# Down projection of eight hidden tiles as seven block products, with their rows kept whole, and a changed last stage

## The chip, the cores and the metric

The kernel runs on one core of one Trainium2 chip. The metric is the device time of one execution in microseconds (us). A core has five engines, each with its own queue that runs in order: TensorE (PE, matmuls into PSUM; PEld is its loading of weights), VectorE (DVE), ScalarE (ACT), GpSimd (POOL) and SyncE (SP, which issues most of the transfers from HBM). They wait for each other through semaphores. TensorE and its accumulators work on tiles of 128 partitions; an accumulator bank of PSUM holds 128x512 numbers of four bytes.

## What is computed

A two-layer trunk over 512 tokens with a model width of 1024. Each layer is a mixer and a gated feed-forward part, each behind an RMS norm and added to the residual. The change touches the feed-forward part of the second layer (layer 1) and the final norm behind it. The feed-forward part has a hidden width of 2816, which is 22 tiles of 128:

```python
def gated_conv_ffn(x, w_gate, w_up, conv_w, conv_b, w_down):
    g = jnp.einsum('bsd,df->bsf', x, w_gate)
    g = causal_dwconv3(g, conv_w) + conv_b
    up = jnp.einsum('bsd,df->bsf', x, w_up)
    return jnp.einsum('bsf,fd->bsd', jax.nn.silu(g) * up, w_down)
...
    h = h + gated_conv_ffn(hn, w_ffn_gate[layer], w_ffn_up[layer], ...)
return rms_norm(h, final_norm)
```

## The kernel before

*Precision.* Every matrix is held as two parts, a rounded high part and the low part that is left (`hi`, `lo`), and every product is three matmuls: high by high, high by low, low by high (`mm3`, L152, recorded at L153, L154 and L155). So each operand must be split. `parts` (L145) does it with a copy on ScalarE (L148) and a subtraction on VectorE (L149); `summed` (L135) does it without VectorE: ScalarE writes the negative of the rounded part (L139), a transfer issued by GpSimd adds the operand onto it in memory (L140), and ScalarE copies the high part (L142). `split` (L257) does the same for rows of activations (L260 on ScalarE, L262 on VectorE), `halves` (L677, recorded at L678 and L679) for sums.

*Rings.* A tile with a tag is one of a fixed number of buffers that are used in turn. Raw weights: four (`raw`, 128x1024, 512 KB each, fetched by SP at L129). Split weights: six (`whi`, `wlo`). Sums: three (`sum`). Activation parts: four (`ahi`, `alo`). Silu rows: three for odd tiles (`s`), two for even ones (`sq`). Whoever takes the next buffer waits until its last reader is done.

*Up projections.* Hidden tiles are taken in pairs f, f + 1; "pair f" below. The gate and up products of a pair are each computed by Strassen's scheme in Winograd's form on two by two blocks: 7 products for the gate and 7 for the up part (`products`, L721), 12 matmuls of 128x256 each (`multiply`, L531, recorded at L542). `prepare` (L681) fetches four raw tiles and makes the weights of all products: a11 is split directly, and s12 and s34 (for g and for u) are sums and differences of blocks which VectorE forms (L698 to L711) and `halves` splits; the fourth block goes through `summed`. The products' order is g1, u1, g5, g6, u5, u6, g2, g7, u2, u7, g4, g3, u4, u3: g1 and u1 need a11, g5 and g6 need s12g, u5 and u6 need s12u, and so on. Results leave PSUM by copies on ScalarE (L736) and adds on VectorE (L741, L746) into padded rows and a tile `kept`; then VectorE multiplies with the norm's factor (L756), convolves (L576), and multiplies silu's result with the up part (L760, L761, L766).

*Down projection.* The rows of four tiles, once split, are multiplied with their 512 columns of the down weights into four banks, one for each 128 tokens, 48 matmuls of 128x512 (`half_down`, L1107), and VectorE adds each bank onto y with the norm's factor (`add`, L1104). A list of steps says which half follows which pair:

```python
    STEPS = [(0, None, True), (2, (0, 2, 0), True), (4, (0, 2, 1), True)]
    for f in range(6, NF, 4):
        STEPS += [(f, (f - 4, f, 0), False), (f + 2, (f - 4, f, 1), f + 4 < NF)]
```
So in layer 1 TensorE runs pair 2, half of tiles 0 and 1, pair 4, their other half, pair 6, half of tiles 2 to 5, pair 8, their other half, pair 10, half of tiles 6 to 9, and so on to pair 20 and the other half of tiles 14 to 17.

*Last four tiles.* Tiles 18 to 21 use the seven-product scheme for the down part too: token halves by tile pairs on one side, tile pairs by column halves on the other. Weights: differences t1, t2 and two more in place (`less`), all seven split by `summed` (`put`). Rows: sums s1, s2 and two in place, each of the seven blocks split into the high and low tiles of the layer's input norm (`hg`), which are free by then. Each product is 12 matmuls of 128x512 for two groups of 128 tokens, recorded at L1204; products 1, 6, 7 and 4 share a bank `a` for each of the two groups, 5 and 3 a bank `e`, 2 has `b`. So the add onto y that reads a bank has to be done before the next product onto that bank begins.

*Order.* A scheduler moves instructions between program order and queue order by due times; `inorder` keeps some in program order, `behind` puts one behind another on its engine. After the last four tiles, the final norm is written out in order by hand: `taken` (a product and its add), `squared` (ScalarE, sum of squares), `halved`, `rooted`, `inverted` (the norm's factor of 128 tokens, on one column), `times` (rows by the norm's gain) and `scaled` (by the factor, and the transfer out).

## Time and profile before

| what | value |
| --- | --- |
| median of three runs | 988.8 us (988.59 to 989.36) |
| the profiled execution | 988.85 us |
| its span in the profile | 987.1 us |
| mean granted TensorE clock | 0.998 of full speed |
| layer 1's pairs 2 to 20 with their down halves | 658.3 to 958.3 us |
| the last four tiles' products, to the last matmul | 958.3 to 977.8 us |
| from there to the end of the span | 9.3 us |
| read from HBM, written | 98.42 MB, 2.10 MB |

The page has, among other parts, the busy time of every engine, the chain of waits that ended last, and groups of instructions by line. A line of a timeline gives an instruction's start in us from the span's start, its duration, engine, line in the kernel, operation, the tiles written and read, and in brackets how long its engine sat idle before it and what ended that. A line of busy time by stretch gives the stretch, its length, then busy time and number of instructions of each engine, the clock, the transfer engines' share and GB/s.

### The profile page before, as it was taken

To read this page: it belongs to the slowest core of one execution; us is meant where nothing else is said; L and a number is where in the kernel's file an instruction comes from. 1 tells how busy PE (TensorE), PEld (TensorE's weight loads), DVE (VectorE), ACT (ScalarE), POOL (GpSimd) and SP (SyncE) were. 2 spreads that over 40 slices of the span, in tenths; PEclk is the share of its full clock that TensorE was granted. 3 is DMA by queue.
4 is the path that set the end of the run, shared out by engine and by line. 5 is a ranking of instruction groups with operands and counts; after the bars stand their busy time and mean duration, and the time that the engine had idled before them with its cause. 6 is when DMAs were issued, how large, how long until landed. Compare 5 with 4: busy or idle time off the path is not lost.

```text
span 987.1 us, 15485 instructions
## 1 busy us (share of the span) xinstructions
PE 975.2 (99%) x6099; PEld 879.9 (89%) x6099; DVE 775.9 (79%) x1181; ACT 562.0 (57%) x843; POOL 112.0 (11%) x129
## 2 busy tenths in 40 slices
PE   9999999999999999999999999999999999999996
PEld 6788888999999999999889988889999999999985
DVE  5797458998788887886887765589987779777787
ACT  5623347755465654655488734576655456554675
POOL 2142022000000000000210001210000000000022
PEclk9999999999999999999999999999999999999999
DMA  7442225555465454653324623264565465445573
GB/s 248 131 150 85 86 86 128 135 137 157 129 150 133 132 142 129 150 130 108 126 64 120 198 69 106 55 140 128 150 166 133 130 149 147 119 135 135 161 151 116
DMA packets 87942, 129.32 MB, mean 131 GB/s; under 512 B 4309, under 2 KB 57789, under 8 KB 87869
## 3 DMA queue, kind: packets, MB, share of 16 engines
q1 hardware_dynamic: 78172, 98.69, 32.2%
q0 software_dynamic: 8208, 27.79, 15.5%
q10 hardware_dynamic: 1488, 1.84, 0.6%
q8 instruction: 48, 0.79, 0.3%
q14 instruction: 26, 0.20, 0.1%
HBM read 98.42 MB, written 2.10 MB: 102 GB/s over the span
## 4 chain that ended last, share of the span: by engine, by line
PE 85%; DVE 8%; ACT 2%; issue 1%; DMA 0%; POOL 0%; ACTq 0%; DVEq 0%
PE dn L153 3%; PE dn L154 3%; PE dn L155 3%; PE d L153 3%; PE d L154 3%; PE d L155 3%; PE oo L155 1%; PE oo L153 1%; PE oo L154 1%; PE oe L154 1%; PE oe L153 1%; PE oe L155 1%; PE u_20a L542 1%; PE u_18a L542 1%; PE u_16a L542 1%
## 5 line engine op out<-in xcount | busy, mean ns | idle before, releaser
L576 DVE SCALAR_TENSOR_TENSOR c<-rows,prm,c 128x512 f32<-128x512 f32 x88 | 64.1, 747 | 1.5 <-ACT c L574 1.4
L140 POOL DMA_DIRECT2D wlo_g<-raw_g x20 | 17.2, 859 | 387.4 <-ACT wlo_g L139 350.4
L153 PE MATMUL d<-a_hi,whi_d 128*128 128x512 f32 x144 | 56.1, 390 | 0.0
L153 PE MATMUL dn<-whi_dn,a_hi 128*128 128x512 f32 x144 | 56.1, 390 | 0.0
L154 PE MATMUL dn<-wlo_dn,a_hi 128*128 128x512 f32 x144 | 56.1, 390 | 0.0
L154 PE MATMUL d<-a_lo,whi_d 128*128 128x512 f32 x144 | 56.1, 390 | 0.0
L155 PE MATMUL d<-a_hi,wlo_d 128*128 128x512 f32 x144 | 56.0, 389 | 0.0
L155 PE MATMUL dn<-whi_dn,a_lo 128*128 128x512 f32 x144 | 56.0, 389 | 0.0
L679 DVE TENSOR_TENSOR wlo_s34u<-s34u,whi_s34u 128x1024 fp32r<-128x1024 f32 x20 | 24.5, 1224 | 25.5 <-ACT whi_s34u L678 25.5
L149 DVE TENSOR_TENSOR wlo_dn<-raw_dn,whi_dn 128x1024 fp32r<-128x1024 f32 x18 | 22.0, 1225 | 23.6 <-ACT whi_dn L148 23.4
L142 ACT ACTIVATE whi_u<-raw_u 128x1024 fp32r<-128x1024 f32 x21 | 22.2, 1055 | 31.6 <-PE d L154 17.5
L149 DVE TENSOR_TENSOR wlo_d<-raw_d,whi_d 128x1024 fp32r<-128x1024 f32 x18 | 22.0, 1224 | 19.5 <-ACT whi_d L148 19.5
L198 ACT ACTIVATE hgh<-h,prm 128x512 fp32r<-128x512 f32 x24 | 17.3, 722 | 35.1 <-DVE h L309 35.0
L140 POOL DMA_DIRECT2D wlo_u<-raw_u x21 | 18.1, 860 | 162.0 <-ACT wlo_u L139 83.7
L584 ACT ACTIVATE s<-c,prm 128x512 f32<-128x512 f32 x44 | 31.2, 714 | 7.3 <-DVE c L576 7.2
L209 POOL TENSOR_TENSOR ssq_f<-ssq_f,sq_f 128x512 f32<-128x512 f32 x14 | 19.7, 1410 | 132.3 <-ACT sq_f L208 97.5
L260 ACT ACTIVATE a_hi<-s 128x512 fp32r<-128x512 f32 x40 | 25.0, 626 | 15.7 <-PE dn L154 9.9
L199 DVE SCALAR_TENSOR_TENSOR hgl<-h,prm,hgh 128x512 fp32r<-128x512 f32 x24 | 23.2, 965 | 12.0 <-ACT hgh L198 11.9
L155 PEld LDWEIGHTS d<-a_hi,wlo_d 128*128 128x128 f32 x144 | 27.0, 188 | 5.7
L155 PEld LDWEIGHTS dn<-whi_dn,a_lo 128*128 128x128 f32 x144 | 27.0, 188 | 5.7
L1104 DVE SCALAR_TENSOR_TENSOR y<-dn,small,y 128x512 f32<-128x512 f32 x40 | 27.7, 748 | 5.5 <-PE dn L155 5.5
L153 PEld LDWEIGHTS d<-a_hi,whi_d 128*128 128x128 f32 x144 | 27.1, 188 | 5.3
(1489 smaller groups left out, 3762.7 us busy)
## 6 DMA issues: line engine op xcount, KB each, us to landing
raw_g<-in_w_ffn_gate_dram SPq DMA_DIRECT2D x40, 512.0 KB, 3.8
raw_u<-in_w_ffn_up_dram SPq DMA_DIRECT2D x40, 512.0 KB, 3.7
raw_dn<-in_w_ffn_down_dram SPq DMA_DIRECT2D x22, 512.0 KB, 3.6
wlo_u<-raw_u POOLq DMA_DIRECT2D x21, 512.0 KB, 5.7
wlo_g<-raw_g POOLq DMA_DIRECT2D x20, 512.0 KB, 4.6
raw_d<-in_w_ffn_down_dram SPq DMA_DIRECT2D x18, 512.0 KB, 3.7
raw_oe<-in_w_out_even_dram SPq DMA_DIRECT2D x8, 512.0 KB, 3.6
raw_v<-in_w_in_odd_dram SPq DMA_DIRECT2D x8, 512.0 KB, 4.5
```

Source lines behind the costliest of these rows:

```text
L140: nc.gpsimd.dma_start(lo, raw, accum_op=ALU.add)
L149: behind(nc.vector.tensor_tensor(lo, raw, hi.bitcast(F32), ALU.subtract), after[0])
L153: nc.tensor.matmul(ps, lhs[0], rhs[0], start=start, stop=False)
L154: nc.tensor.matmul(ps, lhs[0], rhs[1], start=False, stop=False)
L155: nc.tensor.matmul(ps, lhs[1], rhs[0], start=False, stop=stop)
L199: nc.vector.scalar_tensor_tensor(hg[k][1], h[k], g, hg[k][0].bitcast(F32), op0=ALU.mult, op1=ALU.subtract)
L260: nc.scalar.activation(hi, src, AF.Copy, scale=scale)
L542: nc.tensor.matmul(ps, l, r, start=first, stop=end, skip_group_check=True)
L576: nc.vector.scalar_tensor_tensor(c, t[:, i : S + i], prm("cf", i * NF + ft), c, op0=ALU.mult, op1=ALU.add)
L584: nc.scalar.activation(s, c, AF.Silu, bias=self.prm("bf", ft))
L679: nc.vector.tensor_tensor(lo, src, hi.bitcast(F32), ALU.subtract)
L1104: return nc.vector.scalar_tensor_tensor(dst, ps, ffn.cols[:, t : t + 1], dst, op0=ALU.mult, op1=ALU.add)
```

## The change

1. `Ffn` takes a list `apart`; the silu rows of its tiles (6 and 14) lie in the tile that the norm's squares used.
2. The code of the last four tiles becomes a class `Seven`, with which tiles 2 to 5 and 10 to 13 are done as well. Their rows stay whole until all four are there; the blocks' parts lie in the ring of four activation parts, so only four of seven fit at once: blocks 1, 2, 5 and 6 are split when the rows are ready, and blocks 3, 7 and 4 each when products 1, 2 and 5 are done. Of the weights' parts, those of products 3, 7 and 4 are split by `parts` (a copy on ScalarE and a subtraction on VectorE), the other four by `summed`.
3. The list of steps becomes a loop: pair 2, half of tiles 0 and 1, pair 4, their other half, pair 6, the seven products of tiles 2 to 5, pair 8, pair 10, half of tiles 6 to 9, pair 12, their other half, pair 14, the seven products of tiles 10 to 13, pair 16, pair 18, half of tiles 14 to 17, pair 20, their other half, the last four. Between pairs 8 and 10, and 16 and 18, no down part stands.
4. In the last stage three of VectorE's products of rows with the gain go to GpSimd, three scalings change engines, `halved` and two operations of `inverted` take their column operands as scalars (`tensor_scalar`), and the sum of squares of the last 512 columns of tokens 128 to 255 is one operation.

In the built queues the first four matmuls of pair 8 (and 16) stand ahead of product 3 of the block before it, and the rest of the pair behind product 4.

```diff
+            if ft in self.apart:
+                s = tp.tile([P, S], F32, tag="ssq", bufs=1, name=name)
...
+            sevens = (2, 10)
+            ffn = Ffn(1, prm1, norm, ap, sums, [a + 4 for a in sevens])
...
+            class Seven:
...
+                def block(self, product, srcs, home=None):
+                    name = f"dnb{self.a}_{product}"
+                    hi, lo = home or (ap.tile([P, S], F32R, tag=f"a{x}", bufs=4,
+                                              name=f"{name}_{x}") for x in ("hi", "lo"))
...
+                def acts(self, rows, home={}):
...
+                    self.block(1, a11, home.get(1))
+                    self.block(2, a12, home.get(2))
+                    for n in range(2):
+                        nc.vector.tensor_tensor(s1[:, n], a21[n], a22[n], ALU.add)
+                    self.block(5, s1, home.get(5))
+                    for n in range(2):
+                        nc.vector.tensor_tensor(s2[:, n], s1[:, n], a11[n], ALU.subtract)
+                    self.block(6, s2, home.get(6))
+                    for n in range(2):
+                        nc.vector.tensor_tensor(a12[n], a12[n], s2[:, n], ALU.subtract)
+                    for n in range(2):
+                        nc.vector.tensor_tensor(a21[n], a11[n], a21[n], ALU.subtract)
+                    self.rest = [(3, a12, home.get(3)), (7, a21, home.get(7)),
+                                 (4, a22, home.get(4))]
...
+                def weights(self, between, by_vector=()):
...
+                    def put(product, src):
+                        how = parts if product in by_vector else summed
+                        self.stat[product] = how(src, 2, 512, f"dnp{a}_{product}")
...
+                def run(self):
+                    for p in (1, 2, 5, 6, 3, 7, 4):
+                        for i in range(2):
+                            t = i + 2 * (p in (5, 7, 4))
+                            cs = left if p in (1, 2, 4) else right
+                            add(y[t][:, cs], self.product(p, i), t)
+                        if p in (1, 2, 5):
+                            self.block(*self.rest.pop(0))
...
+            for f in range(0, NF, 2):
+                multiplied(f)
+                a = f - 4
+                if part:
+                    part.weights(lambda: None, (3, 7, 4))
+                    part.run()
...
+                    split_rows(f + 1, f)
...
+                elif f - 6 in sevens:
+                    split_rows(f + 1, f)
+                elif f in (2, 4):
+                    half_down(0, 2, f // 2 - 1)
+                elif f % 4 == 2:
+                    half_down(a, f, 0)
+                else:
+                    half_down(a - 2, f - 2, 1)
+                if f > 0 and f % 4 == 0 and f - 2 in sevens:
+                    part = Seven(f - 2)
+                    part.acts(rows)
...
-                inorder(vec.scalar_tensor_tensor(ms, ms, r, r, op0=ALU.mult, op1=ALU.mult))
-                inorder(vec.scalar_tensor_tensor(r, ms, 1.5, r, op0=ALU.add, op1=ALU.mult))
+                inorder(vec.tensor_scalar(ms, ms, r, r, op0=ALU.mult, op1=ALU.mult))
+                inorder(vec.tensor_scalar(r, ms, 1.5, r, op0=ALU.add, op1=ALU.mult))
...
-            times(vec, 2, left)
+            times(pool, 2, left)
...
-            times(vec, 3, right)
+            scaled(vec, 2, left)
             times(pool, 3, left)
...
-            squared(1, right)
+            times(pool, 1, right)
...
+            scaled(vec, 3, left)
+            scaled(pool, 3, right)
```

## The prediction

> **What bounds the kernel now.** I read the page's first part, then busy time by stretch over layer 1's feed-forward, then the timelines of TensorE and VectorE where one step meets the next.

> ```profile
> PE 975.2 (99%) x6099; PEld 879.9 (89%) x6099; DVE 775.9 (79%) x1181; ACT 562.0 (57%) x843; POOL 112.0 (11%) x129
> ```
> TensorE is the bound; VectorE stands at 79% as a mean. What matters is the mean of the stage that changes. The busy time by stretch, cut where pairs 6, 8 and 10 begin (columns: stretch, length, then PE, PEld, DVE, ACT, POOL busy, clock, DMA):

> ```profile
> 709.80:740.80 31.00, 31.00 (x217) 29.11 (x216) 26.93 (x42) 16.69 (x24) 1.72 (x2) 1.00 0.62 158
> 740.80:771.90 31.10, 31.10 (x218) 29.20 (x217) 24.44 (x38) 17.68 (x27) 1.72 (x2) 1.00 0.51 135
> ```
> Each step is a pair's 14 products (12 matmuls each, 1.44 us in the chain of waits, 20.16 us) and one half down part, 10.9 us. TensorE has no gap; VectorE is already busy 87% and 79%. How a down part ends and a pair begins, on TensorE and on VectorE:

> ```profile
> 740.35 0.39 PE L154 MATMUL dn<-wlo_dn,a_hi 128*128 128x512 f32 x1
> 740.58 0.39 PE L155 MATMUL dn<-whi_dn,a_lo 128*128 128x512 f32 x1
> 740.80 0.28 PE L542 MATMUL g_8a<-hgh,whi_a 128*128 128x256 f32 x1
> ```
> ```profile
> 733.48 1.22 DVE L679 TENSOR_TENSOR wlo_s12g<-s12g,whi_s12g 128x1024 fp32r<-128x1024 f32 x1
> 734.61 0.69 DVE L766 TENSOR_TENSOR s<-kept,s 128x512 f32<-128x512 f32 x1
> 735.22 1.23 DVE L679 TENSOR_TENSOR wlo_s34g<-s34g,whi_s34g 128x1024 fp32r<-128x1024 f32 x1
> ...
> 738.96 2.79 DVE L1104 SCALAR_TENSOR_TENSOR y<-dn,small,y 128x512 f32<-128x512 f32 x4 [0.71 <-PE dn L155]
> 741.67 1.22 DVE L679 TENSOR_TENSOR wlo_s12u<-s12u,whi_s12u 128x1024 fp32r<-128x1024 f32 x1
> ```
> A 128x512 matmul issues every 0.227 us. VectorE's paces, from one start to the next in such rows: 1.14 us for 128x1024, 0.60 for 128x512, 0.66 for an add onto y, 0.33 for 128x256. See also where the low part wlo_s12g stands: over six microseconds before the pair that needs it as its third product. That lead is what the change touches.

> **The change, part by part.**

> *Fewer matmuls.* Four tiles' down part was 96 matmuls; seven block products of 12 are 84. Two blocks: 24 x 0.227 = 5.44 us less.

> *More for VectorE.* Per block: weights, 4 differences and 3 low parts at 1.14 where 4 low parts were, +3.4 us; rows, 8 sums of 128x256 and 7 low parts of 128x512 where 4 were, +4.8 us (five of the seven come as two halves); adds onto y, 14 where 8 were, +4.0 us. Together +12.2 us. The two steps above hold 51.4 us of VectorE; 63.6 us would now stand in 62.1 - 2.7 = 59.4 us of TensorE. Other steps have room (24.4 of 31), but rings of six weight tiles and four raw tiles allow little to be done ahead. So VectorE must hold TensorE up there. ScalarE gets +7 copies of 128x1024 at 0.95 and +3 of 128x512 at 0.62, some 8.5 us beside 34 of 62: room as a mean, but it stands in the chain. Bytes from HBM stay; GpSimd issues four accumulating DMAs more per block, with 1.72 us busy per step.

> *Where it is late inside a block.* Let E be the end of pair 6's (or 14's) last product. In the built order VectorE then has, before the add of block product 1 onto y: 0.33 (add of that last product), conv, up and silu multiplies 0.66 + 0.33 + 0.66 + 0.33 + 0.60, two differences of weights 2.28, two low parts 2.28 and the add 0.66 = 8.1 us. Product 6 goes onto the bank that this add reads, and TensorE is there at E + 3 x 2.72 = 8.16: a wait of 0.1 if VectorE was waiting for the last product, more if it came late. It comes late for pair 6: the block's down weights need slots of the raw ring that pair 6's s34u frees, and VectorE reaches those only after the rows' sums (4.5 us) put ahead of wlo_s12u; the last of the three loads lands about 724 (3.6 us from issue in the DMA rows), ScalarE's copy of it, to 725.2, stands ahead of its copy out of PSUM, to 725.5, and VectorE behind that: the two differences t1 and t2 are done at 727.0 and 728.8, and VectorE is at the add of the last product at 731.0, where 730.25 was possible. With ScalarE's silu in between I take 1.0 us for block 2 (ends 0.1 and 1.7) and 0.4 for block 10 (same ends), whose row sums lie beside a 10.9 us down part.
> Then the add's second half 0.66, a low part 1.14, two row blocks 1.33, the adds of product 2 1.32 and the first of product 5 0.66 = 5.1 us. Product 3 goes onto product 5's bank and could begin after product 6 (2.72) and four matmuls of the next pair (0.48): wait 5.1 - 3.2 = 1.9 us (ends 1.2 and 2.2).

> *Where it is late after a block.* In the built order VectorE's sums s12g of the next pair stand behind the last two adds onto y, which wait for the block's last matmul. Let B be the next matmul's issue. By the rows the last add ends at B + 0.87 (741.67 against 740.80); three sums of 128x512 to 2.67; ScalarE's copy, behind one out of PSUM that ends at 2.9, to 3.9; the low part to 5.2. TensorE has 20 matmuls of 0.12 left of the a11 products, is done at 2.4, waits 1.5 for the high part, does four (0.48), waits 0.75 for the low part: 2.25 us in all (ends 1.9 and 2.6). Before, this part was ready six microseconds ahead, so all of it is new. Next in line: wlo_u by DMA, 5.7 us from issue, 0.3 late (ends 0 and 0.5); and pair 10 (18), which now follows pair 8 (16) with no down part between: its s12u stands behind pair 8's convolutions, 0.5 us late (ends 0 and 0.95).

> *Rows kept whole.* s of tiles 6 and 14 in the tile of the norm's squares, free since the norm: nothing, and if it weren't free the silu would wait for it.

> *The tail.* TensorE ends at 977.8 there and VectorE's chain at 982.43.

> ```profile
> 969.34 0.74 DVE L1104 SCALAR_TENSOR_TENSOR y<-dn_a,small,y 128x512 f32<-128x512 f32 x1
> 970.00 0.15 DVE L1229 SCALAR_TENSOR_TENSOR ssf<-ssf 128x1 f32<-128x1 f32 x1
> 970.17 1.29 POOL L1241 TENSOR_TENSOR yf<-y,fin 128x512 f32<-128x512 f32 x1 [7.03 <-DVE ssf L1229]
> ...
> 970.62 0.85 DVE L1237 SCALAR_TENSOR_TENSOR ssf<-ssf 128x1 f32<-128x1 f32 x1
> ```
> ```profile
> 975.76 0.14 DVE L1227 TENSOR_SCALAR ssf<-ssf 128x1 f32<-128x1 f32 x1
> ...
> 977.20 1.03 DVE L1229 SCALAR_TENSOR_TENSOR ssf<-ssf 128x1 f32<-128x1 f32 x1
> ```
> The one-column SCALAR_TENSOR_TENSOR takes 0.15 alone and 0.85 or 1.03 while GpSimd multiplies (970.17 to 971.46), ending as GpSimd ends; a TENSOR_SCALAR of the same size takes 0.14 at 975.76, inside GpSimd's 1.57 us from 975.39. The change makes these TENSOR_SCALAR and takes three 0.60 products off VectorE, but adds two row scalings to it. After the last matmul: adds and the factors of tile 3 to 978.75, the scaling of 3, halving behind ScalarE's square at 979.7, root, inverse, last multiply to 981.5: -0.9. If the scaling waits for GpSimd's own last scaling, to 980.3, the end is +0.1. I take -0.4.
> [...]

> *Sum*, against the profiled execution's own 988.85 (its span 987.1 and 1.75 around it; the median of the runs is 988.8): 988.85 - 5.44 + block 2 (1.0 + 1.9 + 2.25 + 0.3 + 0.5 = 5.95) + block 10 (0.4 + 1.9 + 2.25 + 0.3 + 0.5 = 5.35) - 0.4 = **994.3 us**. All low ends (3.2 a block, tail -0.9): 988.9. All high ends (7.95 a block, tail +0.1): 999.4.

> **Rivals.**
> *VectorE keeps pace* (the other side). If the add of product 5 is through by E + 11.4, the waits inside the blocks vanish and 988.85 - 5.44 + 2 x 2.25 - 0.4 = 987.5 is left; if next pair's s12g is also ready by B + 2.9, 983.0. For it: TensorE shows no wait in the last block, whose 14 adds are alike. Against: that block has a 10.9 us down part ahead of it, no next pair to prepare, and rows for all blocks at once; here 63.6 us of work stand in 59.4.
> *VectorE falls further behind.* The raw slots come free one after another as it goes; if the weights of products 2 and 5 (DMA, 5.7 us after a copy) then land late too, each block loses some 2.5 more: 999.3. For it: in my walk they land within a microsecond of need. Against: TensorE's waits give that time back.
> *The saving does not appear at all:* the built kernel has 24 matmuls fewer, so I give it nothing.

> **How the numbers follow.** Forecast 0.70 (its own range 989.5 to 998); VectorE keeps pace 0.20 (0.13 near 983 to 986.5, 0.07 near 987.5); falls behind 0.10. About 0.2% (2 us) can be told from no change. Faster: 0.13. Same, 986.8 to 990.8: 0.07 and 0.05 from the forecast's low edge, 0.12. Slower: 0.75. The range 987 to 999.5 takes in the bounds and the restart-only case and leaves out the full saving and the worst tenth's upper part.

> **What would show it.** Right: TensorE gaps of one to two microseconds ahead of products 6 and 3, released by adds onto y; 1.5 and 0.75 us ahead of g_8e and g_16e, released by ScalarE's whi_s12g and VectorE's wlo_s12g; VectorE over 90% busy from 711 to 765; the tail's one-column operations all near 0.15. Wrong: a gapless TensorE in pairs 8 and 16, or gaps whose releaser is a DMA (then the second rival), or blocks of 19.0 us.

## The result and the profile after

The changed kernel takes 1003.39 us (median of 4 runs, 1001.93 to 1004.79) against 989.08 for the one before (988.59 to 989.96, 4 runs): ratio 1.0144, 95% interval 1.0132 to 1.0156. The direction was as predicted; the time lies 9.1 us above the forecast and 3.9 above the upper end of its range. The profiled execution took 1004.65, with a span of 1002.8.

The page's first row of the changed kernel, and then the view of all that TensorE waited for over layer 1's feed-forward (total, times, longest). The same view of the kernel before has no row.

```profile
PE 974.6 (97%) x6075; PEld 876.8 (87%) x6075; DVE 797.8 (80%) x1229; ACT 578.9 (58%) x870; POOL 121.6 (12%) x139
```
```profile
PE g_14a L542 <- ACT rows L740: 2.9, 1, 2.9
PE dn_e L1220 <- DVE y L1110: 2.8, 2, 1.4
PE dn_a L1220 <- DVE y L1110: 1.6, 3, 0.8
PE u_10e L542 <- ACT whi_s12u L682: 1.5, 1, 1.5
PE u_18e L542 <- ACT whi_s12u L682: 1.5, 1, 1.5
PE g_16e L542 <- ACT whi_s12g L682: 1.4, 1, 1.4
PE g_8e L542 <- ACT whi_s12g L682: 1.4, 1, 1.4
PE u_16b L542 <- DMA wlo_u<-raw_u: 1.0, 1, 1.0
PE g_10a L542 <- ACT rows L740: 0.9, 1, 0.9
PE g_16e L542 <- DVE wlo_s12g L683: 0.5, 1, 0.5
PE g_8e L542 <- DVE wlo_s12g L683: 0.5, 1, 0.5
```
The 24 matmuls are gone (6075 against 6099), and TensorE has waits at several kinds of places. Counted from the starts of the matmuls, a loss is some 0.15 us longer than its wait in this list (a bracket of 1.42 is 1.58 of lost time). By place, counted so (us):

| where | predicted | after |
| --- | --- | --- |
| matmuls saved | -5.44 | -5.44 |
| inside block 2: waits for adds (products 6 and 3) | 2.9 | 2.6 |
| inside block 2: half the TensorE clock | 0 | 1.6 |
| inside block 10: waits for adds | 2.3 | 2.05 |
| restart after a block (g_8e, g_16e) | 2.25 + 2.25 | 2.26 + 2.26 |
| wlo_u by transfer (pairs 8, 16) | 0.3 + 0.3 | 0.1 + 1.15 |
| pairs 10 and 18 | 0.5 + 0.5 | 2.8 + 2.0 |
| pair 14, ahead of block 10 | 0 | 3.1 |
| last block and the end | -0.4 | +1.0 - 1.5 |

The predicted column adds up to +5.5, the other to +14.0. The 1.8 left of the 15.8 between the profiled executions are some 0.1 us behind each wait, where the next start is late as well, and 0.2 ahead of pair 2.

The restart, as forecast: VectorE's timeline of the changed kernel behind block 2, then TensorE's two waits in pair 8.

```profile
754.32 0.75 DVE L1110 SCALAR_TENSOR_TENSOR y<-dn_a,small,y 128x512 f32<-128x512 f32 x1
754.99 0.68 DVE L702 TENSOR_TENSOR s12g<-raw_g,raw_g 128x512 f32<-128x512 f32 x1
...
758.07 1.22 DVE L683 TENSOR_TENSOR wlo_s12g<-s12g,whi_s12g 128x1024 fp32r<-128x1024 f32 x1
```
```profile
758.09 0.50 PE L542 MATMUL g_8e<-t,whi_s12g 128*128 128x256 f32 x2 [1.42 <-ACT whi_s12g L682]
759.35 0.39 PE L542 MATMUL g_8e<-t,wlo_s12g 128*128 128x256 f32 x1 [0.51 <-DVE wlo_s12g L683]
```
The block's last add ends at 755.07 and only behind it do the sums of the next pair run; in the kernel before, the low part wlo_s12g started at 733.48, seven us ahead of pair 8.

Pair 10, sized too small: ScalarE's and GpSimd's timelines of the changed kernel; SP's, and what SP's queue waited for between 755 and 790; VectorE's and TensorE's timelines.

```profile
760.95 1.05 ACT L139 ACTIVATE wlo_u<-raw_u 128x1024 fp32r<-128x1024 f32 x1
```
```profile
762.30 0.86 POOL L140 DMA_DIRECT2D wlo_u<-raw_u  x1 [10.89 <-PE g_8a L542]
```
```profile
767.97 0.37 SPq L129 DMA_DIRECT2D raw_u<-in_w_ffn_up_dram  x1
```
```profile
SPq L129 <- DMA wlo_u<-raw_u: 6.9, 1, 6.9
```
```profile
774.89 0.69 DVE L702 TENSOR_TENSOR s12u<-raw_u,raw_u 128x512 f32<-128x512 f32 x1 [3.07 <-DMA raw_u<-in_w_ffn_up_dram]
775.50 1.22 DVE L683 TENSOR_TENSOR wlo_s12g<-s12g,whi_s12g 128x1024 fp32r<-128x1024 f32 x1
```
```profile
781.78 0.50 PE L542 MATMUL g_10a<-t,whi_s12g 128*128 128x256 f32 x2 [0.94 <-ACT rows L740]
784.98 0.50 PE L542 MATMUL u_10e<-t,whi_s12u 128*128 128x256 f32 x2 [1.51 <-ACT whi_s12u L682]
```
ScalarE comes to pair 8's fourth up block only at 760.95, behind its copies of the late sums (the first, whi_s12g, at 756.97). So GpSimd's accumulating transfer of that block starts late, at 762.30, and SP waits 6.9 us for the raw slot that it reads from. Only at 767.97 can SP issue the load for pair 10, which takes 6.9 us to land; the prediction had used 3.6 for the block's weights, and no load at all for pair 10. VectorE stands 3.07 us at s12u, with everything of pairs 8 and 10 behind it.

Pair 14, not foreseen: ScalarE's timeline of the changed kernel, the load in its chain of waits, and TensorE.

```profile
850.28 0.37 ACT L740 COPY kept<-u_14a 128x256 f32<-128x256 f32 x1
856.61 1.06 ACT L139 ACTIVATE wlo_dnp<-raw_dn 128x1024 fp32r<-128x1024 f32 x1 [5.96 <-DMA raw_dn<-in_w_ffn_down_dram]
857.57 1.04 ACT L142 ACTIVATE whi_dnp<-raw_dn 128x1024 fp32r<-128x1024 f32 x1
858.51 0.35 ACT L740 COPY rows<-g_14a 128x256 f32<-128x256 f32 x1
```
```profile
850.33 6.25 DMA raw_dn<-in_w_ffn_down_dram
```
```profile
858.92 0.50 PE L542 MATMUL g_14a<-t,whi_g 128*128 128x256 f32 x2 [2.93 <-ACT rows L740]
```
The load of block 10's last down weight is issued at 850.33 and lands 6.25 us later. Here too a raw slot comes late: SP's queue waits 3.3 us for pair 14's own accumulating transfer (wlo_u), which lands at 850.19. ScalarE's copy for product 2 stands in the queue ahead of pair 14's copy out of PSUM, which TensorE's bank needs. The weight is wanted much later; the queue makes it urgent.

The clock, not foreseen either: busy time by stretch of one us in the changed kernel's block 2 (the column before the last two is the granted clock).

```profile
744.00:745.00 1.00, 0.79 (x3) 0.66 (x4) 1.00 (x3) 0.00 (x0) 0.00 (x0) 0.85 0.07 23
745.00:746.00 1.00, 1.00 (x4) 0.81 (x3) 1.00 (x3) 0.00 (x0) 0.00 (x0) 0.50 0.00 0
746.00:747.00 1.00, 1.00 (x4) 0.72 (x4) 1.00 (x3) 0.00 (x0) 0.00 (x0) 0.50 0.00 0
747.00:748.00 1.00, 1.00 (x4) 0.81 (x3) 0.53 (x1) 0.00 (x0) 0.00 (x0) 0.50 0.00 0
```
Product 3's matmuls run at 0.43 us instead of 0.227 for 3.4 us, behind waits of 0.6, 0.4 and 1.6 us. The last 36 matmuls of the block take 9.91 us; in a second profile of the same kernel, with the clock whole, they take 8.31.

### The profile page after: what moved, and what is told of

Read it like the earlier page. It is cut to its first block, busy times and chain, and to the rows that moved or that the text cites. A ratio compares the mean times of both kernels' runs of the same rounds, so it can differ in the third digit from the quotient of the medians.

```text
span 1002.8 us, 15536 instructions
## 1 busy us (share of the span) xinstructions
PE 974.6 (97%) x6075; PEld 876.8 (87%) x6075; DVE 797.8 (80%) x1229; ACT 578.9 (58%) x870; POOL 121.6 (12%) x139
## 3 DMA queue, kind: packets, MB, share of 16 engines
q1 hardware_dynamic: 78172, 98.69, 31.0%
q0 software_dynamic: 9360, 31.99, 17.6%
## 4 chain that ended last, share of the span: by engine, by line
PE 72%; DVE 15%; DMA 3%; ACT 3%; issue 3%; POOL 0%; ACTq 0%; DVEq 0%; POOLq 0%; SPq 0%
PE d L154 3%; PE d L153 3%; PE d L155 3%; DVE y L1110 2%; PE oo L155 1%; PE oo L154 1%; PE oo L153 1%; PE oe L155 1%; PE oe L154 1%; PE oe L153 1%; DMA raw_u<-in_w_ffn_up_dram 1%; PE dn L154 1%; PE dn L153 1%; PE dn_a L1220 1%; PE dn L155 1%
## 5 line engine op out<-in xcount | busy, mean ns | idle before, releaser
L154 PE MATMUL d<-a_lo,whi_d 128*128 128x512 f32 x144 | 56.1, 390 | 0.0
L155 PE MATMUL d<-a_hi,wlo_d 128*128 128x512 f32 x144 | 56.0, 389 | 0.0
L575 ACT ACTIVATE c<-rows,prm 128x512 f32<-128x512 f32 x44 | 31.1, 712 | 8.7 <-DVE rows L760 8.7
L142 ACT ACTIVATE whi_u<-raw_u 128x1024 fp32r<-128x1024 f32 x21 | 22.1, 1054 | 19.1 <-PE d L154 17.6
L155 PEld LDWEIGHTS d<-a_hi,wlo_d 128*128 128x128 f32 x144 | 27.0, 188 | 5.7
L682 ACT ACTIVATE whi_s34u<-s34u 128x1024 fp32r<-128x1024 f32 x20 | 21.2, 1059 | 18.5 <-DVE s34u L715 14.5
L154 PEld LDWEIGHTS d<-a_lo,whi_d 128*128 128x128 f32 x144 | 27.1, 188 | 5.3
L153 PE MATMUL dn<-whi_dn,a_hi 128*128 128x512 f32 x80 | 31.2, 390 | 0.0
L154 PE MATMUL dn<-wlo_dn,a_hi 128*128 128x512 f32 x80 | 31.2, 390 | 0.0
L155 PE MATMUL dn<-whi_dn,a_lo 128*128 128x512 f32 x80 | 31.1, 389 | 0.0
L148 ACT ACTIVATE whi_d<-raw_d 128x1024 fp32r<-128x1024 f32 x18 | 19.0, 1058 | 19.3 <-issue 12.6
```

What stands on the lines that cost most here:

```text
L142: behind(nc.scalar.activation(hi, raw, AF.Copy), first)
L153: nc.tensor.matmul(ps, lhs[0], rhs[0], start=start, stop=False)
L154: nc.tensor.matmul(ps, lhs[0], rhs[1], start=False, stop=False)
L155: nc.tensor.matmul(ps, lhs[1], rhs[0], start=False, stop=stop)
L575: nc.scalar.activation(c, t[:, 0:S], AF.Copy, scale=prm("cf", ft))
L682: nc.scalar.activation(hi, src, AF.Copy)
```

## The experiments

All edits are made to the changed kernel. Times are medians; "before" was 989.1 to 989.25 beside them.

**The tail alone, and one block.**

```diff
-            sevens = (2, 10)
+            sevens = ()        # tail alone
+            sevens = (10,)     # one block
```

> No tiles go through the seven products but the last four; only the last stage is changed. Theory (the blocks cost all of the loss by single waits in the queues; the tail gains what the profile shows, 28.40 us from the last block's first matmul to the end against 28.88): 988.3 us, 0.5 below before. Rival (the tail loses, GpSimd's longer queue of products holds the end): 989.5 or more.

987.74 us (987.32 to 988.09), ratio 0.9984 (0.9975 to 0.9993): the only version faster than the kernel before, by 0.16%. TensorE has no wait in pairs 2 to 20. From the last block's start to the end of the span it is 27.6 us against 28.9 before, so the tail brings 1.3.

> Only tiles 10 to 13 as a block. Theory: the waits of pair 14 (3.1), block 10 (2.1), pair 16 (3.4) and pair 18 (2.0) less 2.7 saved, +7.8, with the tail 0.5: 996.2 us. Rival (the two blocks share one cause that falls on both alike, or on the first alone, such as VectorE's backlog carried from block 2 on): under 994 us, with no wait of 3 us in pair 14.

993.71 (993.14 to 995.81), ratio 1.0049. One block costs 6.0 us net over the tail alone: 8.1 us of waits for 2.72 saved. This is the rival's time: pair 14's wait was 0.8 here, not 3, and most of it comes only with the other block ahead of it. The rival's reason, a backlog of VectorE, does not show: counted from pair 14's first matmul, the third down load is issued at 5.05 with one block as with two, but it takes 4.6 us against 6.3 (4.5 to 4.6 in the three runs with one block, 6.2 to 6.6 in the nine others with two), and the last one lands at 12.8 against 15.1. Why the transfers take longer there is not shown.

**ScalarE's work on product 2's weight behind pair 14's last copy out of PSUM.**

```diff
-                if (key, product) in dst:
-                    nc.scalar.copy(dst[key, product], ps)
+                    self.copied = nc.scalar.copy(dst[key, product], ps)
...
         first = nc.scalar.activation(lo, raw, AF.Copy, scale=-1.0)
+        behind(first, after)
...
+                        more = {"after": ffn.copied} if product == 2 and by_vector else {}
```

> As the changed kernel, but ScalarE's first copy of the weight of block product 2 stands behind the pair's last copy out of PSUM. Theory (in pair 14 the copies out of PSUM were queued behind a copy that waited for a late weight tile, 2.9 us at one matmul): that wait is gone, 1003.4 - 3 = 1000.4 us. Rival (VectorE has too much work there, so a wait that is taken away comes back in the block): within 1 us of 1003.4, block 10 longer by 2 to 3 us.

997.61 (996.77 to 998.71). The pair 14 wait is gone. ScalarE's timeline with this edit:

```profile
854.16 0.37 ACT L741 COPY kept<-u_14a 128x256 f32<-128x256 f32 x1 [2.51 <-PE u_14a L543]
855.60 0.38 ACT L741 COPY rows<-g_14a 128x256 f32<-128x256 f32 x1 [1.07 <-PE g_14a L543]
855.87 1.06 ACT L139 ACTIVATE wlo_dnp<-raw_dn 128x1024 fp32r<-128x1024 f32 x1
```
ScalarE now waits for TensorE here and not for the load. The gain is 5.8 us and not 3, since the profile has no stretch at half clock (1.6; its mean granted clock is 0.998 against 0.996), and u_16b and g_10a wait 0.8 and 0.6 less. The built order now has two matmuls of g_8a and g_16a ahead of product 6, with new waits of 1.5 and 1.3 there; the waits for adds inside the blocks are shorter in turn (0.7 left in block 2, none in block 10, where one of 0.6 for a transfer stands).

**The last product's adds onto y behind the next pair's sums.**

```diff
+                            ps = self.product(p, i)
+                            if p == 4:
+                                ffn.late.append(lambda d=y[t][:, cs], ps=ps, t=t: add(d, ps, t))
+                            else:
+                                add(y[t][:, cs], ps, t)
```
(`late` is emptied in `prepare`, behind the last sum for the gate.)

> As the changed kernel, but the last two adds of a block onto y are put behind the sums s12g and s34g of the next pair. Theory (the 1.4 and 0.5 us ahead of g_8e and g_16e come from these sums standing behind the adds): both waits gone, 2 x 2.2 us, 999.0 us. Rival (VectorE has too much work there): the wait moves to u_8e or the next products, within 1.5 us of 1003.4.

997.01 (995.45 to 997.96). The two waits of pair 8, TensorE's timeline:

```profile
754.65 0.50 PE L542 MATMUL g_8e<-t,whi_s12g 128*128 128x256 f32 x2 [0.23 <-ACT whi_s12g L683]
755.92 0.39 PE L542 MATMUL g_8e<-t,wlo_s12g 128*128 128x256 f32 x1 [0.52 <-DVE wlo_s12g L684]
```
Where it was 1.58 + 0.68 it is 0.39 + 0.68, with a new wait of 0.62 some 20 matmuls on: 1.7 of 2.3 us stay at each of the two places, so the time of 999.0 was beaten by other means. Most of the gain is that the waits of pairs 10 and 18 vanish too, which the expectation had not asked for: pair 8's work ends earlier, so the raw slot is free at 763.8 and not 768.0. The profile (mean granted clock 0.997) has its half-clock stretch in pair 14 instead of block 2.

**Both edits.**

> The two edits in one kernel: the last product's adds of each block behind the next pair's sums s12g (e4: 997.01), and ScalarE's work on block product 2's weight behind the pair's last copy out of PSUM (e3: 997.61). Theory, that the changed kernel's waits are separate places where one late instruction holds a queue, each taken away by its own edit: the gains of 6.4 and 5.8 us add up, less about 1 us where both had taken away the same 2 us of low clock: 992 us (990.5 to 994), with no TensorE gap ahead of g_14a, ahead of g_8e and g_16e at most 0.7 us, and the waits for adds inside the blocks (dn_a, dn_e) still there, 1.5 to 2.2 us a block. Rival, that VectorE's total of work over the blocks is the limit and a wait taken away comes back at the next place: 995.5 to 997.

992.40 (991.99 to 993.35): the gains add up. The rival, that VectorE's total of work is the limit, falls. VectorE's work is the same (796.9 us). Inside the blocks 2.2 and 1.8 us of waits stay, of another kind than expected: as in e3, most of it is g_8a and g_16a waiting for whi_a (1.5 and 1.3).

**The raw slot.** Pairs 8 and 16's fourth blocks without the accumulating transfer:

```diff
+                if self.layer and f in (8, 16):
+                    split_s12()
+                    hi, lo = parts(*raws[key, 1])
```

> As the changed kernel, but the fourth block of pairs 8 and 16's up weights is split by ScalarE's copy and VectorE's subtraction instead of the accumulating transfer, so that its raw slot comes free without waiting for GpSimd's transfer. It gives VectorE one 128x1024 subtraction (1.14 us) more in each of the two pairs. Theory, that the 2.8 and 2.0 us of waits in pairs 10 and 18 come from a raw slot that the late accumulating transfer holds, and with it the late load of the next pair's weights: these waits fall under 0.7 us each, and the time is 999.5 us (998 to 1001). Rival, that VectorE is simply behind by that much at pairs 10 and 18: the subtraction makes it worse by some 1 us in each, 1003.5 to 1006.

The edit takes in the gate's fourth block as well as the up part's, which the expectation left out: VectorE gets 2.3 us more in each pair, not 1.14.

1000.23 (998.96 to 1001.45). Pair 10's load is issued at 763.50 and s12u does not wait (SP's and VectorE's timelines with this edit):

```profile
763.50 0.37 SPq L129 DMA_DIRECT2D raw_u<-in_w_ffn_up_dram  x1
```
```profile
772.65 0.42 DVE L749 TENSOR_TENSOR rows<-g_8e,rows 128x256 f32<-128x256 f32 x1
772.99 0.68 DVE L702 TENSOR_TENSOR s12u<-raw_u,raw_u 128x512 f32<-128x512 f32 x1
```
Pairs 10 and 18 have 0.4 and nothing left of 2.8 and 2.0, though VectorE was given more work. So it is the accumulating transfers, through the slots that they hold, and not VectorE's load.

**More, and less, on VectorE inside the blocks.**

```diff
-                    part.weights(lambda: None, (3, 7, 4))
+                    part.weights(lambda: None, range(8))   # all seven by VectorE
+                    part.weights(lambda: None, ())         # none by VectorE
```

> As the changed kernel, but the other four of the seven weights of each block (products 1, 2, 5 and 6) are also split by ScalarE's copy and VectorE's subtraction, so that a block has no accumulating transfers. VectorE gets 4 x 1.14 = 4.6 us more for each block. Theory, that the blocks' waits are VectorE's: it is behind inside each block and after it, so most of the added time shows: 1003.4 + 2 x 2.5 to 4.6 = 1008 to 1013 us, with gaps ahead of products 6 and 3 longer by 2 us or more, less what the wait ahead of product 1 to pair 10 wins (up to 2 us a block): 1005 to 1012 in all. Rival, that the accumulating transfers are what is late (their own 5 to 7 us, and the loads that share the transfer engines with them): 997 to 1001 us, with shorter loads into the raw ring.

1003.74 (1002.77 to 1006.57), under the theory's bounds and over the rival's. Both were at work: pair 14's wait is gone (the pair takes 20.2 us), but g_8a and g_16a, of which the built order has one or two matmuls ahead of product 6, wait 3.75 and 3.3 us, and half-clock stretches follow both. As a test between the two it is inconclusive.

> The opposite of e7: all seven weights of each block go through the accumulating transfers, so VectorE has three subtractions of 128x1024 (3.4 us) less in each block, and ScalarE three copies and GpSimd three transfers more. In the built order no matmul of the next pair stands between the block's products. Theory, that the waits inside the blocks (for the adds of products 1 and 5) are VectorE's, which is behind by the subtractions that stand ahead of those adds: these waits, 2.6 and 2.05 us, fall under 0.7 in each block; the restart (2.26), pairs 10 and 18 and pair 14 stay: 998.5 us (997 to 1000.5). Rival, that three more transfers of 5 to 7 us come late themselves: waits for transfers of products 3, 7 and 4 take the place, 1002 to 1007.

1000.94 (1000.14 to 1002.58). The waits for the adds of products 1 and 5 vanish, as the theory had it; but block 10 gets a new one, 2.4 us ahead of product 4, followed by some 3.4 us at half clock, and wlo_a is 1.1 late in pair 8, where a second half-clock stretch follows. TensorE's, ScalarE's and VectorE's timelines with this edit:

```profile
878.73 0.47 PE L1220 MATMUL dn_a<-whi_dnp,dnb_hi 128*128 128x512 f32 x1 [2.28 <-ACT wlo_g L139]
```
```profile
876.05 0.63 ACT L682 ACTIVATE whi_a<-raw_u 128x512 fp32r<-128x512 f32 x1 [5.32 <-DMA raw_u<-in_w_ffn_up_dram]
```
```profile
877.23 0.69 DVE L262 TENSOR_TENSOR a_lo<-s,a_hi 128x512 fp32r<-128x512 f32 x1 [2.71 <-ACT a_hi L260]
877.84 0.74 DVE L1110 SCALAR_TENSOR_TENSOR y<-dn_a,small,y 128x512 f32<-128x512 f32 x1
```
The bracket names ScalarE, but the semaphore on which the weight load of this matmul waits is VectorE's, and it moves when the add of product 7 onto y (877.84) is done. That add stood behind a_lo, which waited 2.71 us for ScalarE, and ScalarE had stood 5.32 us for a load of the next pair. The block's own accumulating transfers had all landed by 874.89. So a late load holds TensorE here through two queues, though this product does not need it.

**One block with both edits; and the order of the loads.** The latter brings product 2's weight third instead of fourth:

```diff
-                        for i, j in ((0, 0), (0, 1), (1, 1), (1, 0))}
+                        for i, j in (((0, 0), (0, 1), (1, 0), (1, 1)) if a < NF - 4
+                                     else ((0, 0), (0, 1), (1, 1), (1, 0)))}
```

> One block (tiles 10 to 13) with both edits of e5. From e2 (993.71, with waits of 0.8 ahead of g_14a, 2.26 after the block and 2.16 in pair 18): the first vanishes, the second falls to some 0.7, the third to about 0: 989.4 us (988 to 990.5), so about the time of the kernel before and not under e1's 987.74, since the waits for adds inside the block (2.0 us) and in the last block stay and eat what of the saving of 2.72 is left. Rival, that each wait taken away comes back at the next place: 992 to 993.7.

990.69 (990.04 to 991.78), between the two expectations: g_16a waits 1.3 for whi_a, as in e3, which the expectation had left out.

> As e4 (997.01), and the load of the down weights that product 2 needs is issued third instead of fourth, the one that the second difference needs fourth. Theory, that pair 14's wait of 3.0 us comes from ScalarE's work on product 2's weight standing ahead of its copies out of PSUM while that load is late: the wait vanishes, VectorE's second difference waits instead, behind the pair's adds where there is more time: 994 us (993 to 995.5). Rival, that the late load holds VectorE's queue just as long: 996.5 to 999, with gaps ahead of products 6 and 3 that are longer than in e4.

993.37 (992.62 to 994.69): pair 14's wait gone, and the half-clock stretch behind it (mean granted clock 0.999 against e4's 0.997); the waits inside the blocks are 0.1 to 0.25 us longer than in e4. The late load held ScalarE only because its user stood first in ScalarE's queue.

> One block alone (tiles 10 to 13), with e4's, e9's and e10's edits together. From e1's 987.74: 2.72 less for 12 matmuls, the wait after the block 1.7 (as e4 has left it), 0.9 in the last block (as e2 and e8 have it), waits inside the block 0 to 1: 988.0 us (986.5 to 989.5). Faster than e1 only if what is left of the waits is under 2.7 us.

990.10 (988.83 to 991.29), above the range that was expected. Its profile loses 4.9 us: 2.4 again ahead of block 10's product 4, by the same chain as in e9, some 1.6 at half clock behind it, and waits of 0.6 and 0.3. No version with a block beat the tail alone.

**The changed kernel once more.**

> The changed kernel once more. Its four runs so far lie in two pairs, 1001.9 and 1002.1, 1004.7 and 1004.8, and the profiled one (1004.65) has a stretch of 3.4 us at half the granted clock in block 2, which costs 2.0 us. Theory, that this is not of the kernel's order but of where in time the waits fall: a run without it takes 1002 to 1002.6 us, one with it 1004 to 1005, and the profile agrees with its own run's time. Rival, that every run has it: the profile shows it whatever its time.

1003.42 (1003.41 to 1006.26, 3 runs). The stretch where the first profile had the clock at 0.50, in this one:

```profile
745.00:746.00 1.00, 1.00 (x6) 0.82 (x5) 1.00 (x3) 0.00 (x0) 0.00 (x0) 1.00 0.00 0
746.00:747.00 1.00, 1.00 (x6) 0.82 (x5) 1.00 (x3) 0.65 (x2) 0.00 (x0) 1.00 0.00 0
```
The same three gaps come before it (0.7, 0.3 and 1.58 us), and the clock stays whole: the half clock is not in every execution. The expected 1002 to 1002.6 was missed: u_16b waited 2.5 instead of 1.15, so the lateness of that transfer varies as well. Of the seven executions of this kernel the three longest (1004.65, 1004.79 and 1006.26) are the three whose mean granted clock was under 0.998 (0.996, 0.994 and 0.993). How much of the spread of the times each of the two makes is not shown.

## Why the prediction was right and wrong

*The saving*, 24 matmuls of 0.227: right, 6075 matmuls instead of 6099, and 84 in each block.

*Waits inside the blocks* (2.9 and 2.3): right in place, releaser and size (2.6 and 2.05); the walk along VectorE's queue held. "Block 2 later than block 10" is right by 0.6. e9 takes the waits for products 1 and 5 away by 3.4 us fewer subtractions a block (and the next pair's four matmuls no longer stand between the products).

*Restart* (2.25 each): 2.26 twice, in the two parts forecast. e4 shows the cause of the first part, which falls from 1.58 to 0.39 when the sums stand ahead of the adds. The second part, 0.68, stays in every run with two blocks, so its cause is argued only.

*Pairs 10 and 18* (0.5 each, ends 0 and 0.95): the step that failed. It was costed from VectorE's queue alone (s12u behind pair 8's convolutions), and no load entered it. What decides is the chain one further back: late VectorE, late accumulating transfer, late free slot, late load that in addition takes 6.9 us. The cost was 2.8 and 2.0, above the high end; e6 and e4 bring it down to 0.4 or less by two ways. This is the mechanism of the rival "VectorE falls further behind"; it was put at products 2 and 5, and set aside with the argument that TensorE's waits give the time back. They do not: the slot is held by a transfer that starts only when ScalarE has come round to it.

*Pair 14* (nothing): the step that was missing. The prediction counted ScalarE's added copies as "room as a mean" and looked for loads that land late for the products, where the second rival put them. But the first victim of a late load is what is queued behind its user: pair 14's copies out of PSUM, 3.1 us. e3 and e10 take it away in two ways.

*The clock* (nothing): 1.6 us in that one execution; the median holds some part of it.

*The tail* (-0.4, ends -0.9 and +0.1): -0.5 with the last block's wait of 1.0 in it, -1.3 without (e1), beyond the low end; 0.3 of it lie ahead of the last matmul, which the prediction had not counted. From the last matmul's start to the end of the span it was 9.6 us before and is 8.3. Four scalings change engines there, not three.

The tail's high end, +0.1, had a 128x512 scaling of VectorE wait for GpSimd. The kernel before has rows of one beside GpSimd, early in the trace (VectorE, then GpSimd):

```profile
71.59 0.49 DVE L270 TENSOR_SCALAR cv<-rows,prm 128x512 f32<-128x512 f32 x1
74.31 1.04 DVE L270 TENSOR_SCALAR cv<-rows,prm 128x512 f32<-128x512 f32 x1
```
```profile
73.79 1.29 POOL L498 TENSOR_TENSOR cv<-cv,rstd_m 128x512 f32<-128x512 f32 x1 [9.88 <-PE av L155]
```
Without GpSimd it takes 0.49 us; begun inside GpSimd's product it takes 1.04 and ends 0.28 us behind it, and so does the one at 77.57 (1.02, 0.29 behind). It is held up. In the new last stage (the changed kernel's two timelines) this doesn't show on VectorE, because of where the scaling falls:

```profile
992.98 0.48 DVE L1321 TENSOR_SCALAR y<-yf,ssf 128x512 f32<-128x512 f32 x1
```
```profile
991.79 1.30 POOL L1316 TENSOR_TENSOR yf<-y,fin 128x512 f32<-128x512 f32 x1 [0.37 <-DVE ssf L1311]
993.08 1.54 POOL L1316 TENSOR_TENSOR yf<-y,fin 128x512 f32<-128x512 f32 x1
995.83 1.87 POOL L1321 TENSOR_SCALAR y<-yf,ssf 128x512 f32<-128x512 f32 x1
```
It begins 0.1 us before GpSimd's product ends, and GpSimd's next product, under way with it, takes 1.54 us where its neighbours take 1.30 and 1.27. The second scaling, at 995.78, begins just ahead of GpSimd's own last one and not behind it, so the case that would have given +0.1 did not arise.

*VectorE over 90% busy from 711 to 765*: it was 47.8 of 54.0 us, 89%. *The saving doesn't appear*: rightly given nothing.

In all, the profiled execution lies 10.35 us above the forecast: pairs 10 and 18 (3.8), pair 14 (3.1), the clock (1.6), wlo_u (0.65), less 0.55 inside the blocks and 0.1 in the tail, and 1.8 behind the waits and ahead of pair 2. The median, 9.1 above, has less of the clock.

## What to carry to other kernels

When a step makes an engine late, walk on past the first wait: to the buffer that this engine frees, the transfer that waits for the buffer, the engine that stands in its queue for that transfer, and what is queued behind it there. The waits of pairs 10, 14 and 18 were bystanders', and went away when one instruction or one load was moved or one transfer replaced, with VectorE's and ScalarE's mean load as it was (80% and 58%). A load's time from a stage with quiet transfer queues (3.6 us here) was the low end for the stages in which accumulating transfers ran beside it (up to 6.9).

## What the runs showed of the hardware

Take four traces from 640 us to the last matmul (the changed kernel's first profile, e7, e9 and e11), each cut at such multiples from a half-clock start of its own. Half clock follows each of the five pieces in which TensorE was idle for more than 1.9 us by its records (1.92 and 2.28 in e9, 2.11 in e11, 2.80 and 3.41 in e7), none with less than 1.6, and one of the three between: 1.65 in the changed kernel's block 2, but not 1.68 in e9 and 1.71 in e7. By these traces it matters where the waits fall: the idle time ahead of g_14a in the changed kernel's first profile lies in two pieces, 1.35 and 1.58. How the second profile's three gaps fall into such pieces is not shown.

*Accumulating transfers.* While pair 10's load was under way (767.9 to 775.0), the one accumulating transfer's queue took 51.3% of the transfer engines' time for 0.52 MB, the loads 40.2% for 1.03 MB: 2.5 times as much for a byte. Over the whole run it is 17.6% for 31.99 MB against 31.0% for 98.69 MB, 1.75 times.
